# Keeping only the normalised rows in DRAM between router, expert blocks and combine, with four guessed experts

## The chip, the cores and the metric

The kernel runs on one core of one Trainium2 chip. The metric is the device time of one execution in microseconds; of the kernel before there are three timed runs and one profiled execution. Engine names: PE is the matrix engine (PEld its weight loads), DVE the vector engine, ACT the scalar engine, POOL the general-purpose engine, SP the engine that issues most DMAs. A name with q behind it (SPq, ACTq, POOLq) is that engine's instruction queue.

## The reference, cut to what matters

One decoder layer on 1024 tokens of width 1024: a mixer (gated DeltaNet heads and dilated attention heads), an output projection, a layer norm, a mixture of experts, a second layer norm. The change lies between the first norm and the end:

```python
x = layer_norm(ALPHA * x + (1 + gate1) * mix, ln1_g, ln1_b)
h = x * (1 + scale2) + shift2
lg = h @ w_rg + b_rg                     # 4 groups, the best one is taken
le = h @ w_re + b_re                     # 8 experts in it, the best two are taken
gates = softmax(lg)[grp] * softmax(top2(le))
hid = silu(h @ w_gate[e]) * (h @ w_up[e])   # 32 experts of width 512
y = sum over the two experts of gate * (hid @ w_down[e])
x = layer_norm(ALPHA * x + (1 + gate2) * y, ln2_g, ln2_b)
```

The first norm can be written as xh * ln1_g + ln1_b, where xh is the normalised row. So both h and ALPHA * x are a product and a sum of xh with rows that are the same for all tokens: h = xh * G2 + B2 and ALPHA * x = xh * L1G + L1B.

## The kernel before, in words

**Router stage.** After the mixer, eight tiles of 128 tokens go through two functions, `stage_a(n)` and `stage_b(n - 1)`, in the order `TORD` = 4, 5, 6, 7, 0, 1, 2, 3. `stage_a` finishes the output projection of its tile (`wo_gen`, PE: 48 products of 512 columns, whose moving operands are split in two parts by ACT, L861, and DVE, L863), adds the residual (DVE L1110, L1111), takes mean and variance (DVE L1116 to L1121, with the inverse root by POOL, L448) and writes xh by ACT (L1123). DVE then makes h2 (L1125, L1126), which SP stores to `h2d`; POOL makes ALPHA * x out of xh (L1128, L1129) and stores it to `x1d` (L1130). `stage_b` transposes h2 on PE (L1140), copies it by ACT (L1141), multiplies with the router weights (L128, pc), and `choose` and `places` on DVE (L1015 to L1044) find the two experts of each token and count.

**Guessed experts.** The 32 experts are dealt with in order of how many tokens they have. After four tiles `early` ranks them by what was counted so far; the experts at ranks 4 to 6 (`E0`, `NA` = 3) are loaded while the router still runs: one while the later tiles run, the two others into slots that come free as the stage ends.

**Slot tables.** Then ranks, block bases and slots are worked out (until about 800 us): `idxt` (row to gather per slot), `sct` (row to scatter to), `gat` (gate).

**MoE stage.** 81 static blocks of 32 slots run in the order `SEQ`, each for one expert. A block gathers its rows from `h2d` by POOL (`gather_x`, L1323; a tile of 128x256 holds 32 rows in quarters), PE transposes them (px, L1345), ACT copies (xT), PE multiplies with gate and up (ph, 64 products), ACT and DVE make th (L1359, L1360), PE transposes (pt, L1365), DVE copies (hT, L1367), PE multiplies with down (po, 32 products), DVE applies gate and gate2 (yo, L1378), POOL scatters to `y2d` (L1329). `y2d` has 2048 rows: one per token and choice. The weights stream through four gate/up slots (wgu, 4 MB each) and three down slots (wd, 2 MB each); SP issues a load when the slot's last user on PE is done.

**Surplus loop and end.** A loop (L1433) takes tokens beyond the static blocks; its count is read from memory, and it has no iterations on these inputs. The load of all `x1d` rows (L1486) stands ahead of it; the ln2 rows (L1490) and eight loads of `y2d` rows, 1 MB each (L1511), behind it. `combine` adds the two rows of a token to its x1 row, partly on PE (identity products, L128 ps), partly on DVE (L1517, L1530), ACT squares (L1533), `norm` finishes on DVE (L1540, L1541), and SP writes out (L1542).

A scheduler sets the order on each engine within the program's dependences; pools of buffers (`bufs`) set how far it can go ahead.

Of the kernel before, what the change touches and what calls it, by code (L numbers as in the profile page):

```python
# [20 lines left out]
P = 128  # L21
# [19 lines left out]
def const_tables():  # L41
# [36 lines left out]
    for k in range(2):  # L78
# [5 lines left out]
CAP_BLOCKS = [11, 9, 8, 6, 3, 3] + [2] * 11 + [1] * 12 + [3, 2, 2]  # L84
TE = 4
E0 = 4
NA = 3
# [7 lines left out]
ORDER = [29, 30, 31, 11, 3, 8, 7, 9, 25, 19, 22, 4, 2, 27, 14, 1, 5, 13, 18, 10, 21, 15, 0, 6, 16, 28, 17,  # L95
         12, 20, 26, 23, 24]
SEQ = [1, 1, 2, 2, 3, 3, 0, 0, 0, 5, 5, 4, 6, 6, 4, 7, 7, 4, 8, 4, 9, 4, 4, 10, 11, 11, 11, 12, 12, 12, 13,
       12, 12, 14, 14, 12, 12, 12, 15, 16, 16, 16, 17, 17, 15, 18, 15, 19, 19, 15, 20, 15, 15, 21, 21, 15,
       15, 15, 22, 23, 23, 22, 24, 24, 22, 25, 22, 26, 22, 22, 27, 27, 22, 28, 22, 29, 22, 22, 22, 30, 31]
# [24 lines left out]
def build(nc, tc, I, out):  # L124
# [7 lines left out]
    with es:  # L132
# [15 lines left out]
        h2d = dp.tile([S, D], F32, name="h2d")  # L148
        x1d = dp.tile([S, D], F32, name="x1d")
# [737 lines left out]

        def ln_step(i):
            if i == 1:
                for n_, src in (("G2", modd[2:3, :]), ("l1b", I["ln1_b"]), ("l1g", I["ln1_g"]), ("B2", modd[1:2, :])):  # L890
                    lc[n_] = row(lcp.tile([P, D], F32, name=n_), src)
            if i == LCI[0]:
                sb = lc["sb"] = bp.tile([P, NT, P], F32, name="PT", bufs=2).rearrange("p a b -> p (a b)")
                V.scalar_tensor_tensor(sb, lc["G2"], 1.0, lc["l1b"], op0=OP.add, op1=OP.mult)
                V.tensor_tensor(lc["B2"], lc["B2"], sb, op=OP.add)
            if i == LCI[1]:
                V.scalar_tensor_tensor(lc["G2"], lc["G2"], 1.0, lc["l1g"], op0=OP.add, op1=OP.mult)
            if i == 9:
# [40 lines left out]
        for h in range(H):  # L939
# [3 lines left out]
            if h == H - 1:  # L943
# [8 lines left out]
                lcp = wos.enter_context(tc.tile_pool(name="lcp", bufs=1, side="right", reuse_waits="tile"))  # L952
# [12 lines left out]
        sct = mp.tile([P, NB], I32, name="sct")  # L965
        eidi = mp.tile([1, NE], I32, name="eidi")
# [5 lines left out]
        V.tensor_scalar(g2t, g2t, 1.0, None, op0=OP.add)  # L972
        lt = mp.tile([P, NT, 36], F32, name="lt")
# [119 lines left out]

        def stage_a(n):
# [126 lines left out]
        for o_, c_, p0, p1_ in ((kr, cb, prede[:, 0], prede[:, 1]), (kc_, cc, predc[:, 0:1], predc[:, 1:2])):  # L1221
# [63 lines left out]
        gv = tl([P, 2, NT])  # L1285
# [84 lines left out]
        def block_d(pool, psp, hT, gcol, wd, b_, idx):  # L1370
# [7 lines left out]
            V.scalar_tensor_tensor(yo, po, gcol, g2t, op0=OP.mult, op1=OP.mult)  # L1378
            scatter_y(b_, idx, yo)
# [13 lines left out]
        ngu = nd = NA  # L1393
        fgu, fd = list(range(NA, 4)), list(range(NA, 3))
# [204 lines left out]
```

## Time and profile before

| | us |
|---|---|
| three timed runs | 1355.63, 1357.07, 1357.18 (median 1357.07) |
| the profiled execution | 1359.02 |
| its span | 1357.2 |
| busy in the span: PE, DVE, POOL, ACT | 1201.2, 616.0, 409.3, 335.1 |

The profile belongs to one execution, some 2 us slower than the median; its span is the time between its first and last recorded instruction. A row with a start is one instruction or a run of like ones. `[idle before <-releaser]` says how long the engine had been idle and what ended that. In a chain of work each piece is what the next one waited for, and "issue" is time for which no wait is on record.

### The profile page before, as it was taken

The page shows a single profiled execution, that of the slowest core. Times are in us where ns is not written, and L with a number is a line of the kernel's source. Part 1 is how long each engine was busy: PE and PEld are TensorE (multiplying, and loading weights), DVE is VectorE, ACT ScalarE, POOL GpSimd, SP SyncE. Part 2 cuts the span into 40 slices and gives each one's busy share as a digit, 9 for nine tenths or more (in the row PEclk, how much of TensorE's full clock was granted, in tenths as well). Part 3 has the DMA queues.
Part 4 walks back from the last instruction along what each step waited for, and adds up shares of the span by engine and source line. Part 5 has one row for each costly group of instructions (what it writes and reads, how often), then busy time and mean ns, then how long its engine had stood idle before and what let it go on. Part 6 is the DMA issues. An engine that isn't in the chain of part 4 may idle for free.

```text
span 1357.2 us, 32321 instructions
## 1 busy us (share of the span) xinstructions
PE 1201.2 (89%) x13901; PEld 813.3 (60%) x13901; DVE 616.0 (45%) x1404; ACT 335.1 (25%) x757; POOL 409.3 (30%) x396
## 2 busy tenths in 40 slices
PE   4898999999997989999988459999699999999956
PEld 0476777868785766867766335555355555555522
DVE  0859385674626747577987731111011111111126
ACT  1654343333322333344211101011011111111003
POOL 0223242332223404131532433333233333333113
PEclk8899999999998989999988659999899999999978
DMA  9210001110114335344436859999999999999965
GB/s 378 98 32 33 33 32 34 47 34 17 48 48 134 129 120 162 121 173 110 138 120 250 354 206 420 425 424 423 428 424 411 374 424 422 424 421 423 409 250 220
DMA packets 50629, 311.13 MB, mean 229 GB/s; under 512 B 10226, under 2 KB 18148, under 8 KB 40756
## 3 DMA queue, kind: packets, MB, share of 16 engines
q1 hardware_dynamic: 36064, 282.60, 52.1%
q0 software_dynamic: 8928, 21.00, 4.1%
q10 hardware_dynamic: 5492, 5.44, 1.2%
q8 instruction: 111, 1.82, 0.5%
q14 instruction: 34, 0.28, 0.1%
HBM read 286.56 MB, written 26.89 MB: 231 GB/s over the span
## 4 chain that ended last, share of the span: by engine, by line
PE 40%; DMA 11%; DVE 10%; issue 4%; POOL 3%; ACT 1%; POOLq 0%; SPq 0%; ACTq 0%; DVEq 0%
PE ph L128 17%; PE po L128 9%; DMA wd<-in_k_wd 8%; PE pj L128 5%; DMA araw<-in_w_ada 2%; PE pc L128 2%; PE pg L128 2%; PE pt L1365 1%; DVE acc L259 1%; PE px L1345 1%; POOL wlo L243 1%; DVE oh L1020 1%; DMA y2d<-yo,sct 1%; PE pg L787 1%; ACT sq L1533 1%
## 5 line engine op out<-in xcount | busy, mean ns | idle before, releaser
L128 PE MATMUL ph<-wgu,xT 128*32 128x256 f32 x5184 | 299.0, 383 | 0.0
L128 PEld LDWEIGHTS ph<-wgu,xT 128*32 128x32 f32 x5184 | 160.3, 110 | 113.7 <-issue 16.3
L128 PE MATMUL pj<-hhi,whi 128*128 128x512 f32 x448 | 193.5, 432 | 5.7 <-ACT akq L500 2.4
L128 PE MATMUL pj<-hlo,whi 128*128 128x512 f32 x448 | 181.5, 405 | 3.1 <-DVE hlo L234 2.9
L128 PE MATMUL pj<-hhi,wlo 128*128 128x512 f32 x448 | 180.9, 404 | 0.0
L128 PE MATMUL po<-wd,hT 128*32 128x256 f32 x2592 | 159.1, 387 | 18.0 <-DMA wd<-in_k_wd 17.5
L1323 POOL DMA_INDIRECT xg<-h2d,idxt x81 | 82.6, 1020 | 273.2 <-PE px L1345 265.9
L1360 DVE TENSOR_TENSOR th<-th,ph 128x128 f32<-128x128 f32 x81 | 23.3, 288 | 303.2 <-ACT th L1359 303.2
L243 POOL TENSOR_TENSOR wlo<-wraw,whi 128x256 fp32r<-128x256 f32 x112 | 96.4, 891 | 205.0 <-ACT whi L240 158.5
L128 PEld LDWEIGHTS po<-wd,hT 128*32 128x32 f32 x2592 | 85.5, 112 | 76.6 <-issue 21.2
L1329 POOL DMA_INDIRECT y2d<-yo,sct x81 | 82.0, 1012 | 67.8 <-DVE hT L1367 42.0
L128 PEld LDWEIGHTS pj<-hhi,whi 128*128 128x128 f32 x448 | 85.5, 191 | 23.1 <-ACT akq L500 2.8
L128 PEld LDWEIGHTS pj<-hlo,whi 128*128 128x128 f32 x448 | 85.7, 191 | 20.0 <-DVE hlo L234 7.6
L128 PEld LDWEIGHTS pj<-hhi,wlo 128*128 128x128 f32 x448 | 85.4, 191 | 17.2 <-issue 0.9
L1378 DVE SCALAR_TENSOR_TENSOR yo<-po,gat,g2t 128x256 f32<-128x256 f32 x81 | 39.2, 484 | 115.2 <-PE po L128 115.2
L1359 ACT ACTIVATE th<-ph 128x128 f32<-128x128 f32 x81 | 22.5, 278 | 262.2 <-PE ph L128 262.2
L1347 ACT COPY xT<-px 128x256 f32<-128x256 f32 x81 | 30.2, 373 | 205.0 <-PE px L1345 205.0
L128 PE MATMUL pg<-akq 128*128 128x512 f32 (+3 forms) x96 | 40.7, 539 | 10.2 <-DVE sm L772 6.1
L128 PE MATMUL pj<-wohi,mhi 128*128 128x512 f32 x112 | 46.8, 418 | 0.0
L128 PE MATMUL pj<-wo,mhi 128*128 128x512 f32 x112 | 45.7, 408 | 0.0
L128 PE MATMUL pc<-vtk,PT 128*128 128x128 f32 x288 | 39.2, 281 | 6.6 <-ACT PT L789 6.4
L128 PE MATMUL pj<-wohi,mlo 128*128 128x512 f32 x112 | 45.0, 402 | 0.0
(698 smaller groups left out, 1784.0 us busy)
## 6 DMA issues: line engine op xcount, KB each, us to landing
wgu<-in_k_wgu SPq DMA_DIRECT2D x32, 4096.0 KB, 16.7
wd<-in_k_wd SPq DMA_DIRECT2D x32, 2048.0 KB, 23.7
araw<-in_w_ada SPq DMA_DIRECT2D x32, 512.0 KB, 4.0
wraw<-in_k_win SPq DMA_DIRECT2D x28, 512.0 KB, 3.5
wad<-in_w_ada SPq DMA_DIRECT2D x8, 1024.0 KB, 10.3
wgu<-y2d SPq DMA_DIRECT2D x8, 1024.0 KB, 11.1
xT<-in_k_xt SPq DMA_DIRECT2D x4, 1024.0 KB, 18.4
xr<-in_x SPq DMA_DIRECT2D x8, 512.0 KB, 4.8
```

What stands on the lines that cost most here:

```text
L128: return T.matmul(o, l, r, start=start, stop=stop)
L243: G.tensor_tensor(lo[:, k:k + 2], raw[:, k:k + 2], hi[:, k:k + 2].bitcast(F32), op=OP.subtract)
L259: V.scalar_tensor_tensor(state["acc"], raw, sc[:, k:k + 1], state["acc"], op0=OP.mult, op1=OP.add)
L787: T.transpose(p[:, b_ - b0, :], sc_[:, b_ * P:(b_ + 1) * P], ident)
L1020: V.tensor_scalar(o_, e_, f_, None, op0=OP.is_equal)
L1323: G.indirect_dma_start(out=xg, out_offset=None, in_=h2v, in_offset=bass.IndirectOffsetOnAxis(ap=idx, axis=0), bounds_check=4 * S - 1, oob_ ...
L1329: G.indirect_dma_start(out=y2v[b_], out_offset=bass.IndirectOffsetOnAxis(ap=idx, axis=0), in_=yo, in_offset=None, bounds_check=8 * S - 1, ...
L1345: pe(T.transpose(px[:, hh, :], xg[:, hh * P:(hh + 1) * P], ident))
L1347: A.copy(xT, px)
L1359: A.activation(th, ph[:, 0], AF.Silu)
L1360: V.tensor_tensor(th, th, ph[:, 1], op=OP.mult)
L1378: V.scalar_tensor_tensor(yo, po, gcol, g2t, op0=OP.mult, op1=OP.mult)
```

## The change

1. `h2d` and `x1d` go; SP stores xh alone (`xhd`). DVE's L1125 and L1126 and POOL's L1128, L1129, L1130 go with them, as do the four row loads and their five operations in the attention stage.
2. The router multiplies xh with weights that have G2 folded in, and B2's product is added to the bias (`router_weights`, once).
3. The four rows G2, B2, L1G, L1B are loaded in the blocks' layout (`lns`, sixteen small DMAs by ACT).
4. Each expert block makes h2 out of its gathered xh (`block_h2`) and ALPHA * x (x1 in `block_d`); a block's row that holds a token's first choice (`fst` is 1) gets x1 added to yo. The combine then has two rows to add, not three. xg has 7 buffers in place of 6, yo 4 in place of 7, xT 2 in place of 3; the program gathers 4 blocks ahead in place of 5.
5. Four experts are guessed (`NA` = 4); the fourth one's gate and up weights are loaded into the fourth slot ahead of the MoE stage. `ORDER`, `SEQ` and `CAP_BLOCKS` are new tables of the same kind.
6. The eight `y2d` row loads stand ahead of the surplus loop, and are repeated at the end of each of its iterations. Sums of three of the tiles are made on PE and ACT, of five on DVE.

```diff
-CAP_BLOCKS = [11, 9, 8, 6, 3, 3] + [2] * 11 + [1] * 12 + [3, 2, 2]
+CAP_BLOCKS = [11, 9, 8, 6, 3, 3] + [2] * 10 + [1] * 12 + [3, 2, 2, 2]
-NA = 3
+NA = 4
-SEQ = [1, 1, 2, 2, 3, 3, 0, 0, 0, 5, 5, 4, 6, 6, 4, 7, 7, 4, 8, 4, 9, 4, 4, 10, 11, 11, 11, 12, 12, 12, 13,
+SEQ = [2, 2, 1, 1, 0, 0, 0, 3, 4, 5, 4, 3, 4, 4, 4, 4, 7, 6, 8, 6, 9, 8, 9, 8, 10, 8, 11, 10, 8, 12, 8, 12, 8,
...
+        def ln_consts(k, w):
+            V.scalar_tensor_tensor(w, k[:, G2], 1.0, k[:, L1B], op0=OP.add, op1=OP.mult)
+            V.tensor_tensor(k[:, B2], k[:, B2], w, op=OP.add)
+            V.scalar_tensor_tensor(k[:, G2], k[:, G2], 1.0, k[:, L1G], op0=OP.add, op1=OP.mult)
...
+        def lns_load(j, src):
+            for q in range(4):
+                A.dma_start(lns[32 * q:32 * q + 32, j], src[:, 256 * q:256 * q + 256].to_broadcast([32, 256]))
+        def lns_step(n):
+            if n < 4:
+                lns_load(n, (modd[2:3, :], modd[1:2, :], I["ln1_g"], I["ln1_b"])[n])
...
+        def router_weights():
...
+            V.tensor_tensor(brt, brt, pb[:, 0:36], op=OP.add)
+            V.tensor_tensor(wr[:, :, 0:36], wr[:, :, 0:36], lkc[:, 0, :, None].to_broadcast([P, KD, 36]), op=OP.mult)
...
             A.activation(xh, r_, AF.Identity, bias=mv[:, 4:5], scale=mv[:, 3:4])
-            h2 = lp.tile([P, D], F32, name="h2", bufs=2)
-            V.tensor_tensor(r_, xh, lc["G2"], op=OP.mult)
-            V.tensor_tensor(h2, r_, lc["B2"], op=OP.add)
-            (SY if n < NT - 1 else A).dma_start(h2d[ts, :], h2)
-            G.tensor_tensor(xh, xh, lc["l1g"], op=OP.mult)
-            G.tensor_tensor(xh, xh, lc["l1b"], op=OP.add)
-            G.dma_start(x1d[ts, :], xh)
-            return h2
+            (SY if n < NT - 1 else A).dma_start(xhd[ts, :], xh)
+            return xh
...
+        def block_h2(pool, xg):
+            h2 = pool.tile([P, 256], F32, name="h2", bufs=2)
+            V.tensor_tensor(h2, xg, lns[:, G2], op=OP.mult)
+            V.tensor_tensor(h2, h2, lns[:, B2], op=OP.add)
+            return h2
...
+        def block_d(pool, psp, hT, gcol, wd, b_, idx, xg, fcol):
+            x1 = pool.tile([P, 256], F32, name="x1", bufs=1)
+            V.tensor_tensor(x1, xg, lns[:, L1G], op=OP.mult)
+            V.tensor_tensor(x1, x1, lns[:, L1B], op=OP.add)
...
             V.scalar_tensor_tensor(yo, po, gcol, g2t, op0=OP.mult, op1=OP.mult)
+            V.scalar_tensor_tensor(yo, x1, fcol, yo, op0=OP.mult, op1=OP.add)
...
         down(nb - 1)
+        yall = [ring(fgu[j]).rearrange("p (t k d) -> p t k d", t=4, k=2) for j in range(2)]
+        y2r = y2d.rearrange("(k t p) d -> t p k d", k=2, p=P)
+        def load_rows():
+            for t in range(NT):
+                SY.dma_start(yall[t // 4][:, t % 4], y2r[t])
+        load_rows()
         overflow()
```

What the diff alone doesn't show is where the scheduler puts these instructions. The first place is ACT's queue at the start of the router stage (lns: the new constants; brt: the router's bias; mhi: the split operand of the output projection; hT: the transposed rows). Before:

```order
L970 DMA g2t<-modd 32x256 x4
L1091 DMA brt<-in_b_router_group 128x4
L1092 DMA brt<-in_b_router_expert 128x32
L861 CAST mhi<-mraw 128x896
L1123 ACTIVATE xh<-r__6198,mv 128x1024
L861 CAST mhi<-mraw 128x896
L1141 COPY hT<-pg 128x512 x2
L1123 ACTIVATE xh<-r__6255,mv 128x1024
```

and now:

```order
L1079 DMA brt<-in_b_router_expert 128x32
L1095 DMA lns<-modd 32x256 x4
L860 CAST mhi<-mraw 128x896
L1147 ACTIVATE xh<-r__6191,mv 128x1024
L1095 DMA lns<-modd 32x256 x4
L1095 DMA lns<-in_ln_g 32x256 x4
L1095 DMA lns<-in_ln_b 32x256
L860 CAST mhi<-mraw 128x896
L1095 DMA lns<-in_ln_b 32x256
L1159 COPY hT<-pg 128x512 x2
L1095 DMA lns<-in_ln_b 32x256 x2
L1147 ACTIVATE xh<-r__6262,mv 128x1024
```

Four of the sixteen loads now stand ahead of the first tile's cast and xh, ten ahead of its hT copies, and the others ahead of the second tile's xh. Each waits on one of eight semaphores that SP's and ACT's DMAs share in turn.

The second place is DVE in the middle of the MoE stage, one block and a half. Before:

```order
L1378 SCALAR_TENSOR_TENSOR yo<-po,gat,g2t 128x256
L1367 COPY hT<-pt 128x128
L1360 TENSOR_TENSOR th<-th,ph 128x128
L1378 SCALAR_TENSOR_TENSOR yo<-po,gat,g2t 128x256
L1367 COPY hT<-pt 128x128
```

and now (h_ is h2 of the block two ahead, x_ the x1 of the block whose yo comes next):

```order
L1424 SCALAR_TENSOR_TENSOR yo<-po,gat,g2t 128x256
L1409 COPY hT<-pt 128x128
L1425 SCALAR_TENSOR_TENSOR yo<-x_10105,fst,yo 128x256
L1380 TENSOR_TENSOR h_10235<-xg,lns 128x256
L1415 TENSOR_TENSOR x_10194<-xg,lns 128x256
L1381 TENSOR_TENSOR h_10235<-h_10235,lns 128x256
L1416 TENSOR_TENSOR x_10194<-x_10194,lns 128x256
L1402 TENSOR_TENSOR th<-th,ph 128x128
L1424 SCALAR_TENSOR_TENSOR yo<-po,gat,g2t 128x256
L1409 COPY hT<-pt 128x128
```

Five operations have come between hT and the next th.

The third place is SP at the end, from the last weight load on (wgu names the slot that is reused for the rows). Before:

```order
L1486 DMA wgu_13347<-x1d 128x8x1024 [waits DMAHW2_49]
L1433 COMPARE_AND_BRANCH
L1433 UNCONDITIONAL_BRANCH
...
L1490 DMA wd_13545<-in_ln_g 128x1024
L1490 DMA wd_13545<-in_ln_b 128x1024
L1511 DMA wgu_13869<-y2d 128x2x1024 [waits DMASW5_49]
```

and now:

```order
L1544 DMA wd_14087<-in_ln_g 128x1024 [waits DMAHW3_49,PE_49]
L1544 DMA wd_14087<-in_ln_b 128x1024 [waits DMAHW2_49]
L1560 DMA wgu_14182<-y2d 128x2x1024 [waits DMASW4_49,DMASW5_49,DMASW3_49,DMASW6_49,DMASW2_49,DMASW7_49,DMASW1_49,DMASW0_49]
L1560 DMA wgu_14182<-y2d 128x2x1024 [waits DMAHW4_49]
...
L1483 COMPARE_AND_BRANCH
L1483 UNCONDITIONAL_BRANCH [waits DMAHW0_49,DMAHW1_49,DMAHW2_49,DMAHW3_49,DMAHW4_49,DMAHW5_49,DMAHW6_49,DMAHW7_49]
```

The row loads stand ahead of the loop's branches; the branch that goes round the loop (the second row of L1483) now waits on all eight semaphores of SP's DMAs, where it had no wait before. On POOL the last eight scatters now stand ahead of its loop branches, where the last one stood behind.

## Rows read from the trace of the kernel before

**Rows 1.** Windows: stretch, length, busy per engine (instructions), clock, DMA share, GB/s

```profile
675.25:692.50 17.25, 15.02 (x77) 12.01 (x76) 14.64 (x33) 3.36 (x4) 7.01 (x5) 0.90 0.34 119
785.00:800.00 15.00, 5.23 (x34) 4.81 (x34) 6.38 (x17) 0.00 (x0) 3.48 (x8) 0.50 0.20 87
815.00:1265.00 450.00, 435.71 (x7361) 248.19 (x7357) 72.57 (x225) 48.35 (x149) 148.60 (x146) 0.98 1.00 418
```

**Rows 2.** Chain of work in the router stage: start, length, piece

```profile
698.48 1.40 PE pg L1140 x8
750.33 3.41 POOL xh L1128
757.94 0.58 POOL mv L448
768.84 1.93 PE pc L128 x16
```

**Rows 3.** Timelines of DVE and POOL in one router tile: start, length, instruction

```profile
691.94 2.38 DVE L1017 SCALAR_TENSOR_TENSOR e<-lem,m,kc 128x32 f32<-128x32 f32 x1
695.05 1.72 DVE L1020 TENSOR_SCALAR oh<-e,f__6646 128x32 f32<-128x32 f32 x1
697.25 0.25 DVE L1017 SCALAR_TENSOR_TENSOR e<-lem,m,kc 128x32 f32<-128x32 f32 x1
690.84 3.43 POOL L1128 TENSOR_TENSOR xh<-xh,l1g 128x1024 f32<-128x1024 f32 x1 [4.42 <-DVE r__6522 L1125]
```

**Rows 4.** ACT's g2t loads by line (ns min/median/max), then its timeline

```profile
L970 ACTq DMA_DIRECT2D g2t<-modd x4: 432/444/1971, 635.0 to 638.0; - x4
635.01 3.39 ACTq L970 DMA_DIRECT2D g2t<-modd  x4
639.40 0.94 ACT L861 CAST mhi<-mraw 128x896 fp32r<-128x896 f32 x1 [5.22 <-DMA g2t<-modd]
```

**Rows 5.** Timelines in the MoE stage: PE (start, then one block), DVE, POOL

```profile
802.41 0.66 PE L1345 MATMUL px<-kc,xg 128*128 128x128 f32 x2 [5.23 <-DMA xg<-h2d,idxt]
1003.30 0.33 PE L1365 MATMUL pt<-kc,th 128*128 128x128 f32 x1
1009.10 0.33 PE L1365 MATMUL pt<-kc,th 128*128 128x128 f32 x1
1002.02 0.29 DVE L1360 TENSOR_TENSOR th<-th,ph 128x128 f32<-128x128 f32 x1 [3.70 <-ACT th L1359]
1004.12 1.02 POOL L1323 DMA_INDIRECT xg<-h2d,idxt  x1 [3.45 <-PE px L1345]
1005.45 1.01 POOL L1329 DMA_INDIRECT y2d<-yo,sct  x1 [0.31 <-issue]
```

**Rows 6.** PE's waits in the stage, SP's first loads, gathers from issue to landing

```profile
PE po L128 <- DMA wd<-in_k_wd: 17.5, 5, 9.9
804.98 9.88 SPq L988 DMA_DIRECT2D wgu<-in_k_wgu  x2
DMA to landing us min/median/max: 2.7/9.4/11.9
```

**Rows 7.** The end: DVE's and SP's timelines, the chain, groups of operations

```profile
1300.76 0.48 DVE L1378 SCALAR_TENSOR_TENSOR yo<-po,gat,g2t 128x256 f32<-128x256 f32 x1 [2.06 <-PE po L128]
1314.20 1.23 DVE L1517 TENSOR_TENSOR wgu<-wgu 128x1024 f32<-128x1024 f32 x1 [12.96 <-DMA wgu<-y2d]
1309.34 6.67 SPq L1511 DMA_DIRECT2D wgu<-y2d  x8
1303.54 5.78 DMA y2d<-yo,sct
1351.14 1.28 DVE wgu L1541
L1540 DVE SCALAR_TENSOR_TENSOR wgu<-wgu,mv,wd 128x1024 f32<-128x1024 f32 x8 | 10.2, 1281 | 0.0
L1530 DVE CUSTOM_DVE_ANT_0 wgu<-wgu,wgu 128x1024 f32<-128x1024 f32 x2 | 2.4, 1223 | 0.0
```

More of the change, by code (lines that the diff above doesn't have):

```diff
@@ L147, in build @@
         modd = dp.tile([4, D], F32, name="modd")
-        h2d = dp.tile([S, D], F32, name="h2d")
-        x1d = dp.tile([S, D], F32, name="x1d")
+        xhd = dp.tile([S, D], F32, name="xhd")
         y2d = nc.dram_tensor("y2d", [2 * S, D], F32)[:, :]
@@ L965, in build @@
         sct = mp.tile([P, NB], I32, name="sct")
+        fst = mp.tile([P, NB], F32, name="fst")
         eidi = mp.tile([1, NE], I32, name="eidi")
@@ L972, in build @@
         V.tensor_scalar(g2t, g2t, 1.0, None, op0=OP.add)
+        lns = mp.tile([P, 4, 256], F32, name="lns")
+        G2, B2, L1G, L1B = range(4)
         lt = mp.tile([P, NT, 36], F32, name="lt")
@@ L1092, in build @@
         A.dma_start(brt[:, 4:36], I["b_router_expert"].to_broadcast([P, 32]))
+        lnk = lp.tile([KD, 4, P], F32, name="lnk")
+        for j, src in enumerate((modd[2:3, :], modd[1:2, :], I["ln1_g"], I["ln1_b"])):
+            SY.dma_start(lnk[:, j], src.rearrange("o (k p) -> (o k) p", p=P))
+        lnw = lp.tile([P, 256], F32, name="lnw")
+        def ln_consts(k, w):
+            V.scalar_tensor_tensor(w, k[:, G2], 1.0, k[:, L1B], op0=OP.add, op1=OP.mult)
+            V.tensor_tensor(k[:, B2], k[:, B2], w, op=OP.add)
+            V.scalar_tensor_tensor(k[:, G2], k[:, G2], 1.0, k[:, L1G], op0=OP.add, op1=OP.mult)
+        ln_consts(lnk, lnw[0:KD, 0:P])
+        def lns_load(j, src):
[4 more added lines that the diff above has]
+                lns_load(n, (modd[2:3, :], modd[1:2, :], I["ln1_g"], I["ln1_b"])[n])
+            if n == 6:
+                ln_consts(lns, lnw)
+                V.tensor_scalar(lns[:, L1G:L1B + 1], lns[:, L1G:L1B + 1], ALPHA, None, op0=OP.mult)
+        def router_weights():
+            pk = pch()
+            for j, c_ in ((G2, 0), (B2, KD)):
+                T.transpose(pk[:, c_:c_ + KD], lnk[:, j], ident[0:KD, 0:KD])
+            lkc = lp.tile([P, 2, KD], F32, name="lkc")
+            V.tensor_copy(lkc, pk[:, 0:2 * KD].rearrange("p (j k) -> p j k", j=2))
+            pb = pch()
+            for k in range(KD):
+                mm(pb[:, 0:36], lkc[:, 1, k:k + 1].to_broadcast([P, P]), wr[:, k, 0:36], start=(k == 0), stop=(k == KD - 1))
+            V.tensor_tensor(brt, brt, pb[:, 0:36], op=OP.add)
+            V.tensor_tensor(wr[:, :, 0:36], wr[:, :, 0:36], lkc[:, 0, :, None].to_broadcast([P, KD, 36]), op=OP.mult)
         def stage_a(n):
@@ L1177, in build @@
             h2n = stage_a(n)
+            if n == 0:
+                router_weights()
+            lns_step(n)
             if n > 1:
@@ L1195, in build @@
         wpools["wgu2"] = wpools["wd2"] = wqb
-        for i in range(1, NA):
+        for i in range(1, 3):
             load_gu(i, i, eid_reg(eide, E0 + i))
             load_d(i, i)
+            if i == 2:
+                wqc = mes.enter_context(tc.tile_pool(name="wqc", bufs=1, side="right", reuse_waits="tile"))
+                wpools["wgu3"] = wqc
+                load_gu(3, 3, eid_reg(eide, E0 + 3))
         rts = ExitStack()
@@ L1284, in build @@
         V.scalar_tensor_tensor(gs[:, 2], gs[:, 1], 1.0, gs[:, 0], op0=OP.add, op1=OP.mult)
-        gv = tl([P, 2, NT])
+        gv = rtk.tile([P, 2, NT], F32, name="gv")
         V.reciprocal(gv[:, 0], gs[:, 2])
@@ L1392, in build @@
         b0s = [b_ // BT_ for b_ in BASES]
-        ngu = nd = NA
-        fgu, fd = list(range(NA, 4)), list(range(NA, 3))
+        ngu, nd = NA, NA - 1
+        fgu, fd = [], []
         left = [CAP_BLOCKS[r] for r in ORDER]
@@ L1446, in overflow @@
                 V.tensor_copy(gcl[:, 0:1], pc_[:, 1:2])
+                first(gcl[:, 3:4], ic[:, 3:4], ic[:, 0:1])
                 V.tensor_scalar(gcl[:, 1:2], ctr, float(-NB), None, op0=OP.add)
@@ L1464, in build @@
             G.memset(xp_.tile([P, 256], F32, name="xg", bufs=XB), 0.0)
-        for n in range(XB - 1):
+        for n in range(LG):
             gx(n)
@@ L1483, in build @@
                     break
-            if nd == NE and fgu and xall is None:
-                xall = ring(fgu.pop(0)).rearrange("p (t d) -> p t d", d=D)
-                SY.dma_start(xall, x1d.rearrange("(t p) d -> p t d", p=P))
             if nd == NE and fd and lnb is None:
```

113 lines of the change are left out of this document (51 added, 62 removed).

## The prediction

> **What bounds the kernel now.** I read the windows by stage first, then the chain of work through the router stage, then single engines' timelines where a term needs one. The windows [rows 1] show four regimes. In the router stage (633 to 769 us) a steady token tile takes 17.25 us, in which PE is busy 15.02 at clock 0.90 and DVE 14.64: neither is full, so the two wait for each other. In the MoE stage (802 to 1301) PE is busy 435.71 of 450 us while the DMA share is 1.00 at 418 GB/s: two limits at nearly the same height. In the last 56 us (1301 to 1357) the row loads and then DVE's operations of 1.28 us set the pace [rows 7]. The slot tables between (769 to 802) are a chain of small operations that the change leaves as it is.
>
> The chain through the router [rows 2] shows what the tile waits for: the transposes of h2 (PE pg L1140) stand behind DVE and POOL, and in the later tiles POOL's L1128 (3.41 us at 750.33) lies in the chain itself, with POOL's small mv (757.94) waiting its turn behind it. DVE's rows [rows 3] show why DVE is so full: L1017 takes 2.38 us while POOL's L1128 runs, and 0.25 us with POOL free; L1020, of the same kind, takes 1.72 beside L1129.
>
> **The change part by part.** The profiled execution took 1359.02 us with a span of 1357.2, so 1.8 lie around the span; it stands 1.95 above the median of 1357.07. I sum against the span, and take the difference from the median at the end.
>
> *Router stage, removed.* Each tile loses DVE L1125 and L1126 (2 x 1.2 us), POOL L1128 (3.43 us), L1129 and the x1d issue, and the stretch of L1017 and L1020, (2.38 - 0.25) + (1.72 - 0.25) = 3.6 us [rows 3]. L1125 and L1126 are costed by the combine's sum of the same size, 1.23 us [rows 7]. DVE falls from 14.6 to 14.6 - 2.4 - 3.6 = 8.6 us a tile, so PE is late next. PE's 15.02 us at clock 0.90 would be 13.5 at the full 2.4 GHz [rows 1]; I take 14.3 a tile, midway. That is 2.95 less than 17.25. From the transposes of the fourth tile at 698.48 to the last router product at 768.84 [rows 2] are 70.4 us for four tiles, so 4 x 2.95 = 11.8; in the last tile mv no longer stands behind the previous tile's POOL pair, 750.33 to 757.94 or 7.6 us instead of one tile's 2.95, so 4.7 more. The three tiles before give 3 x 2.95 = 8.9.
>
> *Router stage, added.* The eight loads of G2 and B2 rows become small: four by SP and sixteen of 32x256 (lns) on ACT's queue. The nearest row: g2t's four issues have a median of 0.444 us and a longest of 1.97, and ACT's next cast waited 5.22 us [rows 4]. Behind the sixteen stand, on ACT, the casts of mhi for the output projection, xh and the hT copies; PE waits for these. Four lie before the first cast and xh(0), ten before hT(0). Bounds: 16 x 0.444 = 7 us and 16 x 1.97 = 32; I take 0.85 each (g2t's four from 635.01 took 3.39), which makes hT(0) some 7 us late (twelve to fourteen issues, less the wait of ACT that they fill), less 2.4 as h2 is gone: about 5 us once. The router weights (two transposes, eight products, two DVE operations) cost about 1 us, under the same stall. So the stage ends 11.8 + 4.7 + 8.9 - 5 - 1 = 19.4 us sooner; I take 18, since some waits on DVE stay, and bounds of 8 (the pace shrinks by one operation only) and 24 (no stall). The constants' work taken out of the last attention stretch, on DVE, ACT and SP, is hidden beside PE: 0 to 3, I take 1.
>
> *Fourth guessed expert.* Its 4.19 MB are read in the gap before the MoE stage, where DMA moves 87 GB/s [rows 1]: 10.0 us at the 418 GB/s of the stage behind it, free if it ends before the first gathers, up to 3 us if not; I take 1.5. The start of the stage also gets h2's two products, x1's first and a seventh memset: four operations of 0.3 to 0.5, 1.5 us. Together +3.
>
> *MoE stage.* PE's pace is 5.80 us a block (1003.30 to 1009.10, [rows 5]), 81 blocks or 469.8 us; the stage took 498.3, from the first px at 802.4 [rows 5] to the last po at 1300.7, just ahead of the last yo [rows 7]. Of the other 28.5 us po waited 17.5 for wd [rows 6]; about 11 are a first block at half clock, slower clock behind the stalls, and the end. The transfers, 182.5 MB of weights (29 experts of 6.29 MB) and 21.2 MB of gathered and scattered rows (162 of 0.131), need 487 us at 418 GB/s: the stalls are those of a stream with little slack. After, 4.19 MB less are to come, but the stream starts later: before, a slot was free and it began at 804.98 [rows 6]; after, all four slots are full, and the first comes free when the first expert's two blocks have left gate and up, about 8.3 us into the stage. 8.3 + 199.5/0.418 = 486: the saving and the late start nearly cancel at the floor, but the work in hand at the start is one expert more, which covers early stalls. I expect 11 to 12 us of stalls in place of 17.5: -6, bounds -10 and +3.
>
> Five DVE operations of 128x256 come into each block (h2, x1, and the sum into yo), at about 0.33 each, between th's 0.29 [rows 5] and yo's 0.48 [rows 7]: 1.65 us. In each block DVE is idle 3.70 us before th [rows 5], so they fit. The scatter leaves 0.33 us later and the gather stands behind x1; with gathers landing in at most 11.9 us [rows 6] and seven buffers, four blocks or 23 us lie between issue and use. Cost 0.
>
> What the DVE rows do beside POOL [rows 3] speaks against this cover: POOL issues a gather and a scatter, 1.02 and 1.01 us, in just that idle stretch [rows 5]. Two holds of that length make 1.65 + 2.03 = 3.68 of 3.70 us, so still free, and th, done at 1002.31, has another 1.0 us until its transpose at 1003.30. The Trainium skill, "SBUF — State Buffer", section "SBUF: two separate sides", says that an operation with two SBUF inputs and one on GpSimd exclude each other for the whole instruction; that agrees with L1017, and no row here shows it for a DMA issue. It would take effect only with longer holds; that is rival 4.
>
> *The end.* Before, the last scatter stood behind the surplus loop: yo was done at 1301.24, the scatter issued at 1303.54, landed 5.78 us later, and the row loads began at 1309.34 [rows 7]. After, the scatter stands before the loop: yo's end, r (0.33), issue and landing give 1307.4. But all eight loads now stand before the loop too, and on the way round it SP waits for all eight and the exit holds every engine for SP. So the combine that began at 1314.20 with the first rows [rows 7] can't begin until 8.39 MB have landed: 20.1 us at 418 GB/s and 1 to start, 1328.5; through the loop another 2.3 (as 1301.24 to 1303.54 before), 1330.8. By the Trainium skill, "DMA: Bandwidth & Descriptors", section "Where 436 GB/s comes from", reads from HBM are held to about 358 GB/s, which would make these loads 23.4 us and the end 3.3 later; the 418 GB/s held over 450 us [rows 1] speak against it, and the sum keeps 418. Then DVE's own work is left bare: 16 operations of 1.28, five sums of 1.22 [rows 7], and sixteen tiny ones of about 0.15, 29 us, with first and last steps on ACT and POOL 32: 1362.8. From the last DVE operation (1351.14 + 1.28) to the end are 4.8 us: 1367.6 against 1357.2, +10. Bounds +5 (the combine's DVE packs without gaps, a quick loop) and +14.
>
> *Sum:* -1 - 18 + 3 - 6 + 10 = -12: span 1345, own time 1347, and 12 below the median: **1345 us**.
>
> **The rivals.**
> 1. *The loop doesn't hold the combine*: the wait at SP's branch may concern earlier transfers only. Then the end is 2 us sooner than before in place of 10 later: 1333. For it: nothing runs between loads and combine that needs the loop. Against: the order of SP shows the wait on all eight lanes of its queue, which before hadn't one.
> 2. *ACT's sixteen issues cost more than the router gains.* Place: ACT ahead of xh(0) and hT(0). At 1.97 us each [rows 4], fourteen take 28 instead of 12 us, 15 net more: 1360, slower than before. It decides from about 1.7 us an issue. For it: each waits for an earlier transfer of its lane. Against: g2t's median.
> 3. *The MoE stage gains nothing*: the late start of the stream eats the saved bytes, +0 to +3 in place of -6: 1351 to 1354.
> 4. *Holds between DVE and POOL in the MoE stage.* If an issue holds DVE as long as L1017 was held, 2.13 us, a block has 1.65 + 4.26 = 5.9 for 4.7 of room: 1.2 x 81 = 97 us, less 15 of stalls it hides: about 1427. Against it: the issues themselves last 1.0 us [rows 5], half of that. What the Trainium skill says in the section cited above is its mechanism.
> 5. *The router tiles keep their pace*: DVE's chain of small operations sets it, not the big ones, and only 8 are won: 1355, no change to speak of.
>
> **How the numbers follow.** Forecast 0.57, rivals 0.10, 0.10, 0.13, 0.03 and 0.07 in that order. The range reaches from rival 1 to just short of rival 2: 1333 to 1358, since the bounds of router (-24 to -8), MoE (-10 to +3) and end (+5 to +14) seldom all fall on one side. A measurement of this kernel tells 0.2% (2.7 us) from no change. Faster: the forecast, rival 1, nearly all of 3, a little of 5, 0.80. Same: most of 5 and a bit of 2 and 3, 0.07. Slower: 2, 4, and the forecast's worst corner, 0.13.
>
> **What would show it.** Router: tiles at 14 to 14.5 us with L1017 at 0.25 throughout, and the last router product near 750. A first tile with ACT held over 15 us on lns would be rival 2. MoE: th still waited for by ACT alone, stalls on wd under 15 us, block pace 5.80. End: a stretch of some 20 us with no engine busy while rows land, and DVE then at over 90%. I am wrong if DVE starts the combine within 15 us of the last po, if the router's tiles stay over 16 us, or if po waits for wd over 25 us.

## The result: 25 us faster, twice the forecast

| | us |
|---|---|
| kernel before, median | 1357.09 |
| changed kernel, four runs | 1331.42, 1331.80, 1332.42, 1334.79 (median 1332.11) |
| ratio, 95% interval | 0.9828 [0.981, 0.9846] |
| profiled execution of the changed kernel, its span | 1331.80, 1329.6 |

The direction was right. The size was not: 25 us against the 12 forecast, and the median lies 0.9 us under the low end of the stated range. The spans differ by 27.6 us, the medians by 25.0 (the profiled execution of the kernel before is 2 us above its median). Four marks divide the spans (the last router product on PE, the first px, the first operation on the last yo, the end):

| piece | before | after | difference | forecast |
|---|---|---|---|---|
| to the last router product | 768.8 | 738.8 | -30.0 | -19 |
| from there to the first px | 33.6 | 37.6 | +4.0 | +3 |
| MoE stage, to the last yo | 498.4 | 491.1 | -7.2 | -6 |
| from there to the end | 56.4 | 62.1 | +5.7 | +10 |

So the two middle pieces came out near the forecast in size. The router gave 11 us more, and the end took 4 us less.

### The profile page after: what moved, and what is told of

Same layout as the page of the kernel before. It is cut to its first block, busy times and chain, and to the rows that moved or that the text cites. A ratio compares the mean times of both kernels' runs of the same rounds, so it can differ in the third digit from the quotient of the medians.

```text
span 1329.6 us, 32637 instructions
## 1 busy us (share of the span) xinstructions
PE 1175.5 (88%) x13879; PEld 802.4 (60%) x13879; DVE 712.3 (54%) x1802; ACT 331.6 (25%) x753; POOL 377.3 (28%) x373
## 5 line engine op out<-in xcount | busy, mean ns | idle before, releaser
L1365 POOL DMA_INDIRECT y2d<-yo,sct x81 | 102.6, 1267 | 287.3 <-DVE yo L1425 287.3
L128 PEld LDWEIGHTS po<-wd,hT 128*32 128x32 f32 x2592 | 85.8, 111 | 70.4 <-issue 11.3
L1402 DVE TENSOR_TENSOR th<-th,ph 128x128 f32<-128x128 f32 x81 | 23.3, 288 | 164.6 <-ACT th L1401 164.6
L1359 POOL DMA_INDIRECT xg<-xhd,idxt x81 | 83.8, 1035 | 26.1 <-issue 25.9
L447 POOL TENSOR_TENSOR mv<-mv,pio 128x1 f32<-128x1 f32 x16 | 14.4, 900 | 142.4 <-DVE mv L1143 86.3
L258 DVE SCALAR_TENSOR_TENSOR acc<-araw,sc,acc 128x1024 f32<-128x1024 f32 x28 | 37.5, 1339 | 14.0 <-DMA araw<-in_w_ada 13.9
```

Source lines behind the costliest of these rows:

```text
L128: return T.matmul(o, l, r, start=start, stop=stop)
L258: V.scalar_tensor_tensor(state["acc"], raw, sc[:, k:k + 1], state["acc"], op0=OP.mult, op1=OP.add)
L447: G.tensor_tensor(o, x, e.to_broadcast(list(x.shape)), op=OP.pow)
L1359: G.indirect_dma_start(out=xg, out_offset=None, in_=xhv, in_offset=bass.IndirectOffsetOnAxis(ap=idx, axis=0), bounds_check=4 * S - 1, oob_ ...
L1365: G.indirect_dma_start(out=y2v[b_], out_offset=bass.IndirectOffsetOnAxis(ap=idx, axis=0), in_=yo, in_offset=None, bounds_check=8 * S - 1, ...
L1402: V.tensor_tensor(th, th, ph[:, 1], op=OP.mult)
```

## The profile after

First the marks, on PE's timeline of the changed kernel (start, length, instruction): the transposes of two tiles that follow each other, the last router product, the first px.

```profile
674.23 1.07 PE L1158 MATMUL pg<-kc,xh 128*128 128x128 f32 x8
687.69 1.07 PE L1158 MATMUL pg<-kc,xh 128*128 128x128 f32 x8
738.75 1.98 PE L128 MATMUL pc<-hT,wr 128*64 128x128 f32 x16
776.35 0.66 PE L1387 MATMUL px<-kc,h 128*128 128x128 f32 x2 [9.50 <-DVE eidi L1526]
```

The tiles follow each other at 13.46 us, where the steady tile of before took 17.25 [rows 1].

Then the start of the router, on PE's timelines: the last transposes of the attention stage and the router's first, before, and the same two now, with the products of the router weights between.

```profile
632.82 0.63 PE L811 MATMUL pg<-kc,ob 128*128 128x128 f32 x4 [1.10 <-DVE ob L807]
646.94 1.03 PE L1140 MATMUL pg<-kc,h 128*128 128x128 f32 x8
```

```profile
630.81 0.63 PE L810 MATMUL pg<-kc,ob 128*128 128x128 f32 x4 [1.10 <-DVE ob L806]
639.59 1.95 PE L128 MATMUL pc<-wr,lkc 128*128 128x36 f32 x16 [0.18 <-issue]
647.60 1.04 PE L1158 MATMUL pg<-kc,xh 128*128 128x128 f32 x8
```

So the 30.0 us of the first piece have three parts. The stage begins 2.0 us sooner, but nothing can be read from that: in the nine profiled kernels that have the changed kernel's code up to there it begins anywhere from 628.5 to 636.6. Its first transposes come 16.8 us after that start in place of 14.1, or 2.7 later, with PE busy all the way (14.00 of the 14 us from 633 in the kernel before, 16.82 of the 17 from 631 now). From the first transposes to the last product are 91.2 us in place of 121.8, a gain of 30.7 in the tiles.

The windows of the changed kernel (columns as in [rows 1]) show the steady tile, the MoE stage and the stretch after the last scatter.

```profile
675.25:692.50 17.25, 17.13 (x103) 13.52 (x102) 12.67 (x37) 4.04 (x6) 0.54 (x1) 1.00 0.35 114
805.00:1230.00 425.00, 413.29 (x6993) 236.47 (x6985) 190.18 (x563) 45.88 (x142) 162.69 (x141) 0.99 1.00 416
1268.00:1295.00 27.00, 0.00 (x0) 0.00 (x0) 0.48 (x1) 0.00 (x0) 0.98 (x1) 0.55 0.79 313
```

In the same 17.25 us PE is busy 17.13 where it had 15.02, and the clock is 1.00 where it was 0.90 [rows 1]; POOL's 7.01 us of work are down to 0.54. In the last window no engine computes more than next to nothing for 27 us (DVE 0.48, POOL's 0.98 is the last scatter's issue). DVE's short operation that took 2.38 us beside POOL [rows 3] (now L1004, ns min/median/max) is never held:

```profile
L1004 DVE SCALAR_TENSOR_TENSOR e<-lem,m,kc x16: 250/252/255, 655.7 to 744.9; 128x32 f32<-128x32 f32 x16
```

The end, on DVE's, POOL's and SP's timelines, and two windows of it:

```profile
1267.48 0.48 DVE L1424 SCALAR_TENSOR_TENSOR yo<-po,gat,g2t 128x256 f32<-128x256 f32 x1 [1.51 <-PE po L128]
1295.04 1.23 DVE L1583 CUSTOM_DVE_ANT_0 wgu<-wgu 128x1024 f32<-128x1024 f32 x1 [26.56 <-SPq L1483]
1324.58 1.28 DVE L1593 SCALAR_TENSOR_TENSOR wgu<-wgu,mv,wd 128x1024 f32<-128x1024 f32 x1
1268.76 0.98 POOL L1365 DMA_INDIRECT y2d<-yo,sct  x1 [2.38 <-DVE yo L1425]
1271.76 4.91 SPq L1560 DMA_DIRECT2D wgu<-y2d  x8
1276.00:1292.00 16.00, 0.00 (x0) 0.00 (x0) 0.00 (x0) 0.00 (x0) 0.00 (x0) 0.50 1.02 417
1294.00:1295.00 1.00, 0.00 (x0) 0.00 (x0) 0.00 (x0) 0.00 (x0) 0.00 (x0) 0.50 0.00 0
```

The row loads are issued 4.3 us after the last yo begins, but DVE waits 26.56 us, and what it waits for is SP at the loop's line. That is the wait that the order of SP showed. The rows move at 417 GB/s, and by 1294 no transfer is left; only then, at 1295.04, DVE begins. Before, DVE began as the first rows landed [rows 7].

In the MoE stage, PE's wait for down weights and one stretch of DVE and POOL:

```profile
PE po L128 <- DMA wd<-in_k_wd: 13.0, 6, 4.8
1034.41 0.29 DVE L1402 TENSOR_TENSOR th<-th,ph 128x128 f32<-128x128 f32 x1 [1.96 <-ACT th L1401]
1031.38 1.28 POOL L1365 DMA_INDIRECT y2d<-yo,sct  x1 [3.18 <-DVE yo L1425]
```

Po's 17.5 us of waits [rows 6] are 13.0 now. DVE is idle 1.96 us before th, where it was 3.70 [rows 5], so the five operations take 1.74. The scatter's issue takes 1.28 us where it took 1.01 [rows 5].

## Experiments

### Which of the removed operations freed the router

Theory: POOL's two long operations held DVE and the small mv. Rival: DVE's own two operations were the load. Three kernels: the first takes only POOL's pair out of the kernel before, the second only DVE's, the third puts a POOL pair back into the changed kernel (a shorter one: 1.9 and 2.4 us, where the removed pair took 3.4 and 2.4).

e2_before_no_pool, on the kernel before:

```diff
-            G.tensor_tensor(xh, xh, lc["l1g"], op=OP.mult)
-            G.tensor_tensor(xh, xh, lc["l1b"], op=OP.add)
```

e3_before_no_h2, on the kernel before:

```diff
-            V.tensor_tensor(r_, xh, lc["G2"], op=OP.mult)
-            V.tensor_tensor(h2, r_, lc["B2"], op=OP.add)
-            (SY if n < NT - 1 else A).dma_start(h2d[ts, :], h2)
-            G.tensor_tensor(xh, xh, lc["l1g"], op=OP.mult)
-            G.tensor_tensor(xh, xh, lc["l1b"], op=OP.add)
-            G.dma_start(x1d[ts, :], xh)
-            return h2
+            (SY if n < NT - 1 else A).dma_start(h2d[ts, :], xh)
+            G.tensor_tensor(h2, xh, lc["l1g"], op=OP.mult)
+            G.tensor_tensor(h2, h2, lc["l1b"], op=OP.add)
+            G.dma_start(x1d[ts, :], h2)
+            return xh
```

e7_pool_back, on the changed kernel:

```diff
+            px_ = lp.tile([P, D], F32, name="px_", bufs=1)
+            G.tensor_tensor(px_, xh, xh, op=OP.mult)
+            G.tensor_tensor(px_, px_, xh, op=OP.add)
```

e2_before_no_pool, expected:

> The kernel before without POOL's two operations on xh (L1128, L1129) in the router stage: the residual's constants are left out, and x1d gets xh itself. Theory (POOL's long operations stretch DVE's and hold back mv, and the clock is low because PE waits): tile period from 17.25 to 14.6 us or less, clock above 0.95, the last router product 12 to 25 us earlier, total 1332 to 1345. Rival (DVE's own two operations of 128x1024 are the bound): 0 to 5 us faster, 1352 to 1357.

e3_before_no_h2, expected:

> The kernel before without DVE's two operations on xh (L1125, L1126): h2 is xh, so the second scale and shift are left out; POOL's two operations stay (they write a tile of their own). Theory (POOL is the larger part): DVE still stretched, tile period 15 to 16.5 us, 3 to 10 us faster in all, 1347 to 1354. Rival (DVE's own work is the bound): 12 us or more faster, under 1345.

e7_pool_back, expected:

> The changed kernel with two POOL operations of 128x1024 put back into each router tile, reading xh and writing a tile that nobody reads. Theory (POOL's operations were what slowed the router): 8 to 20 us slower than the changed kernel, 1340 to 1352, with L1004 at over 2 us in each tile and a clock under 1.0 in the stage. Rival (with DVE's two operations gone there is room enough): under 3 us slower, below 1335.

Measured: 1330.37 us (ratio to before 0.9774 [0.9753, 0.9795]), 1376.51 (1.0118 [1.0098, 1.0139]) and 1344.98 (0.9885 [0.9858, 0.9911]). First e2, PE's timeline (first transposes, last product) and a window in the steady tiles:

```profile
645.84 1.03 PE L1138 MATMUL pg<-kc,h 128*128 128x128 f32 x8
740.39 1.77 PE L128 MATMUL pc<-hT,wr 128*64 128x128 f32 x16
660.00:690.00 30.00, 29.86 (x176) 23.65 (x175) 25.40 (x70) 7.45 (x10) 2.26 (x4) 1.00 0.41 139
```

Without POOL's pair alone the last product is at 740.4: 28.4 of the router's 30 us (27.3 of the 30.7 in the tiles), more than the 12 to 25 expected. The clock is 1.00, and the total is no longer than that of the changed kernel (0.9774 of the kernel before, against 0.9828). DVE's two operations still run there, so taking them away adds little once POOL is out. No short operation on DVE is held in e2; how much of the gain is theirs and how much is that of the small mv behind POOL's pair was not separated.

Then e3 and e7, each with the first transposes and the last product on PE; of e3 the instruction that tells why its total can't be read (a group by line: count, busy, mean ns), and of e7 the transposes of the fourth and the fifth tile, two waits of PE, DVE's L1007 in one tile and the window around the fifth tile.

```profile
646.50 1.03 PE L1138 MATMUL pg<-kc,xh 128*128 128x128 f32 x8
751.20 1.98 PE L128 MATMUL pc<-hT,wr 128*64 128x128 f32 x16
L1452 POOL DMA_INDIRECT wgu<-in_k_wgu,ic x1 | 1.0, 982 | 4.5 <-DMA wgu<-x1d 4.5
```

```profile
649.72 1.03 PE L1161 MATMUL pg<-kc,xh 128*128 128x128 f32 x8
691.49 1.07 PE L1161 MATMUL pg<-kc,xh 128*128 128x128 f32 x8
705.13 0.18 PE L128 MATMUL pc<-Mc,onesb 128*128 128x32 bf16 x1 [3.46 <-DVE Mc L1024]
712.97 1.07 PE L1161 MATMUL pg<-kc,xh 128*128 128x128 f32 x8
751.87 0.19 PE L128 MATMUL pc<-Mb,striub 128*128 128x32 bf16 x1 [4.60 <-DVE Mb L1020]
752.01 1.98 PE L128 MATMUL pc<-hT,wr 128*64 128x128 f32 x16
687.25 2.20 DVE L1007 TENSOR_SCALAR oh<-e,f__6659 128x32 f32<-128x32 f32 x1
690.00:720.00 30.00, 26.41 (x138) 19.72 (x137) 21.70 (x68) 6.52 (x8) 5.36 (x5) 0.89 0.41 156
```

In e3 the last product is 17.6 us earlier than before, at 751.2 (17.1 in the tiles). Its total is longer because h2 without scale and shift sends tokens to other experts: the surplus loop ran once (L1452 is in its body). Only its router stage is evidence. The steady tiles follow each other at 14.0 us (674.47 to 688.47), where 15 to 16.5 were expected, and 17 us is more than the theory's 3 to 10 and lies where the rival had it: DVE's own two operations were a load nearly as large as POOL's pair. The larger part is POOL's, as stated, but only by 27 to 17.

In e7 the last product is at 752.0, 13.3 later than in the changed kernel, of which 2.1 lie ahead of the first transposes and 11.1 in the tiles; the total is longer by 8 us (by the ratios) to 13 (by the medians), as the theory had it. L1007, of the same kind as the L1020 of before, is held 2.20 us again, and L1004 in seven of its sixteen instances, but the steady tiles still follow each other in 13.5 us: with DVE's pair gone there is room for the hold. What is lost is lost mainly at two places. The fifth tile, ahead of which four tiles' counts are ranked, comes 21.5 us after the fourth (712.97 after 691.49; 15.2 in the changed kernel), and PE waits there 3.46 us for the held chain on DVE. At the last tile PE waits 4.60 us for the chain of small operations. So the savings overlap: in the tiles POOL's pair 27, DVE's pair 17, both 31.

### ACT's sixteen issues

```diff
-                A.dma_start(lns[32 * q:32 * q + 32, j], src[:, 256 * q:256 * q + 256].to_broadcast([32, 256]))
+                SY.dma_start(lns[32 * q:32 * q + 32, j], src[:, 256 * q:256 * q + 256].to_broadcast([32, 256]))
```

> The changed kernel with the sixteen small lns loads issued by SP instead of ACT. Theory (ACT's queue delays the first tile's hT by little, PE has other products to run): 0 to 2 us faster, 1330 to 1333. Rival (ACT's queue holds the router's start, as the prediction had it with 5 us): 3 to 6 us faster, 1326 to 1329.

Measured: 1335.05 us, 0.982 [0.9794, 0.9847]; the changed kernel's 0.9828 lies inside. The last transposes of the attention stage and the router's first (630.81 and 647.60 in the changed kernel):

```profile
630.98 0.63 PE L810 MATMUL pg<-kc,ob 128*128 128x128 f32 x4 [1.10 <-DVE ob L806]
647.61 1.04 PE L1158 MATMUL pg<-kc,xh 128*128 128x128 f32 x8
```

The way between the two is 16.6 us in place of 16.8, and the last product (738.75 and 738.89) did not move either. In the changed kernel ACT's sixteen issues had taken 0.31 to 0.78 us each, a median near 0.43, and PE was busy 29.01 of the 30 us from 630 to 660: it had other products to run. The 5 us of the prediction for this queue were 0.

### The MoE stage

Four kernels. One loads the fourth guessed expert late; one goes back to three guessed experts with the orders of before; one leaves out the five DVE operations; one does four of them twice.

e4_gu3_late:

```diff
-                load_gu(3, 3, eid_reg(eide, E0 + 3))
...
+        load_gu(3, 3, eid_reg(eidi, ORDER[3]))
         for n, (i, b_) in enumerate(blocks):
```

e8_three_guessed, which also has CAP_BLOCKS, ORDER and SEQ of before:

```diff
-NA = 4
+NA = 3
...
-                load_gu(3, 3, eid_reg(eide, E0 + 3))
...
-        ngu, nd = NA, NA - 1
-        fgu, fd = [], []
+        ngu = nd = NA
+        fgu, fd = list(range(NA, 4)), list(range(NA, 3))
```

e5_lean_blocks:

```diff
-            V.tensor_tensor(h2, xg, lns[:, G2], op=OP.mult)
-            V.tensor_tensor(h2, h2, lns[:, B2], op=OP.add)
-            V.tensor_tensor(x1, xg, lns[:, L1G], op=OP.mult)
-            V.tensor_tensor(x1, x1, lns[:, L1B], op=OP.add)
-            V.scalar_tensor_tensor(yo, x1, fcol, yo, op0=OP.mult, op1=OP.add)
```

e9_double_ops, and the same for the two operations on x1:

```diff
             V.tensor_tensor(h2, xg, lns[:, G2], op=OP.mult)
             V.tensor_tensor(h2, h2, lns[:, B2], op=OP.add)
+            V.tensor_tensor(h2, xg, lns[:, G2], op=OP.mult)
+            V.tensor_tensor(h2, h2, lns[:, B2], op=OP.add)
```

e4_gu3_late, expected:

> The changed kernel, but the fourth guessed expert's gate and up weights are loaded at the start of the MoE stage (with the numbers the gathers wait for), not in the gap ahead of it. Theory of the prediction (one expert more in hand is worth 6 us to the stage and costs 3 to 4 at its start): the way to the first px gets 3.5 us shorter, the stage 6 longer, total about 1335. Rival (saved bytes and late start of the stream cancel): the stage stays within 1 us, total about 1329.

e8_three_guessed, expected:

> The changed kernel with three guessed experts, and with the orders, caps and first loads of the kernel before; the rest of the change stays. The late load of the fourth expert's weights cost the MoE stage only 0.5 us, so the 7 us that the stage won lie elsewhere. Theory (the new block order and the fourth guess together): the stage, first px to last yo, goes back to 496 to 499 us from 491, the waits of po for wd to 17 us, total 1336 to 1340. Rival (the x1d reads and the shorter scatter traffic that are gone): the stage stays at 490 to 492, total 1330 to 1333.

e5_lean_blocks, expected:

> The changed kernel without the five added DVE operations of each expert block: blocks use the gathered normalised rows as they are and the residual is not added to yo, so that part of the computation is left out. Theory (they lie in DVE's idle time): total 1330 to 1333, the MoE stage within 2 us of 491. Rival (holds between DVE and POOL, or the later scatters, cost the stage): 3 us or more faster.

e9_double_ops, expected:

> The changed kernel with h2 and x1 of each block computed twice, so four more DVE operations of 128x256 a block, some 1.35 us where 1.96 us of DVE's idle time are left ahead of th. Theory (the added operations lie in idle time): the stage within 2 us of 491, total 1330 to 1334. Rival (DVE's operations or holds with POOL cost the stage part of their length): 10 us or more slower.

Measured: 1333.76, 1336.78, 1331.56 and 1335.05 us; ratios 0.9822, 0.9816, 0.98 and 0.9814, with intervals that all hold the changed kernel's 0.9828. So the totals do not decide, and the stage's own marks must (first px and the operation on the last yo; stage in the changed kernel 776.35 to 1267.48, 491.1 us). How far such marks move by themselves is seen in e1, e6, e7 and e10, which have the changed kernel's tables, gap and blocks: with the changed kernel, their stages are 489.7 to 491.2 us, and from the last router product to the first px are 36.7 to 37.8.

e4, timelines of PE and DVE and the wait of po:

```profile
775.86 0.66 PE L1386 MATMUL px<-kc,h 128*128 128x128 f32 x2 [8.36 <-DVE eidi L1525]
1267.46 0.48 DVE L1423 SCALAR_TENSOR_TENSOR yo<-po,gat,g2t 128x256 f32<-128x256 f32 x1 [1.79 <-PE po L128]
PE po L128 <- DMA wd<-in_k_wd: 11.5, 5, 4.0
```

491.6 us: the early load of the fourth expert is worth 0.5 us to the stage. The way to the first px got 0.75 us shorter (36.8), not 3.5. Both are no more than the spread of kernels that have the early load, so no price of it is seen: the saved bytes and the late start of the stream cancel, as the rival had it. The rival's total of 1329 did not come, as it had counted on the 3.5.

e8, the same rows:

```profile
781.13 0.66 PE L1386 MATMUL px<-kc,h 128*128 128x128 f32 x2 [8.22 <-DVE eidi L1525]
1278.54 0.48 DVE L1423 SCALAR_TENSOR_TENSOR yo<-po,gat,g2t 128x256 f32<-128x256 f32 x1 [0.80 <-PE po L128]
PE po L128 <- DMA wd<-in_k_wd: 17.8, 7, 9.7
```

497.4 us, and the wait is back at 17.8. So of the 7 us that the stage won, 6 come with the new tables and the fourth guess together, and by e4 not through the time at which the fourth expert is loaded. That leaves the tables of caps and order; but they were not put back alone, so this is a conclusion by subtraction, and which entry does it was not tried. (The router stage of this run began 5.7 us later than that of the changed kernel, so only its MoE stage is compared.)

e5 and e9, the last yo of each, of e5 PE's wait, a block on PE, and its scatters by line (ns min/median/max), and of e9 the first px and a gather's issue:

```profile
1266.85 0.48 DVE L1418 SCALAR_TENSOR_TENSOR yo<-po,gat,g2t 128x256 f32<-128x256 f32 x1 [2.25 <-PE po L128]
PE po L128 <- DMA wd<-in_k_wd: 1.1, 2, 0.8
1002.06 0.33 PE L1404 MATMUL pt<-kc,th 128*128 128x128 f32 x1
1007.95 0.33 PE L1404 MATMUL pt<-kc,th 128*128 128x128 f32 x1
L1365 POOL DMA_INDIRECT y2d<-yo,sct x81: 980/1017/1028, 794.0 to 1267.6; - x81
```

```profile
1030.57 1.30 POOL L1359 DMA_INDIRECT xg<-xhd,idxt  x1 [0.72 <-DVE x L1419]
775.49 0.66 PE L1389 MATMUL px<-kc,h 128*128 128x128 f32 x2 [10.59 <-DVE h L1383]
1268.18 0.48 DVE L1428 SCALAR_TENSOR_TENSOR yo<-po,gat,g2t 128x256 f32<-128x256 f32 x1
```

e5's stage is 489.8 us from its first px at 777.01, e9's 492.7 from 775.49. Four more operations in each of 81 blocks, some 110 us of DVE's time, cost 1.6 us, hardly more than the spread: the theory holds, the added operations lie in idle time. In e5 po hardly waits, but its blocks take 5.89 us on PE in place of 5.80, so no more is won than 1.3 us, within the spread. Why they take longer, with the clock at 1.00, stays open.

### The end

e1_rows_behind; the first line taken out is the call at the end of an iteration of the surplus loop:

```diff
-                load_rows()
...
-        load_rows()
         overflow()
         xes.close()
+        load_rows()
```

e10_rows_behind_sums has the same and this, by which PE and ACT, not DVE, make the sums of two more tiles:

```diff
-        ASUM = (1, 3, 5)
+        ASUM = (1, 2, 3, 5, 6)
```

e1_rows_behind, expected:

> The changed kernel with one thing undone: the eight row loads stand behind the surplus loop again, as they did before. Theory (the loop holds the combine until all rows have landed): DVE starts the combine within 15 us of the last yo instead of 27.6, the end shrinks from 62 us to about 53, total about 1323 us. Rival (loads ahead of the loop are a gain, and the end is long because of the combine's own work): the loads start 4 to 5 us later, total 1334 to 1337.

e10_rows_behind_sums, expected:

> The changed kernel with the row loads behind the loop, as in e1_rows_behind, and five of the eight sums of the combine on PE and ACT in place of three. Theory (with rows streaming in, DVE's own 30 us set the end): DVE loses two sums of 1.3 us, 1 to 3 us faster than e1_rows_behind. Rival (the landing of the rows sets it, or ACT becomes late): within 1 us of it, or slower.

Measured: 1316.68 us, 0.9697 [0.9665, 0.9729], and 1320.79, 0.9695 [0.9655, 0.9735]. e1's timelines of SP and DVE:

```profile
1266.27 0.48 DVE L1424 SCALAR_TENSOR_TENSOR yo<-po,gat,g2t 128x256 f32<-128x256 f32 x1 [1.77 <-PE po L128]
1276.67 1.23 DVE L1582 CUSTOM_DVE_ANT_0 wgu<-wgu 128x1024 f32<-128x1024 f32 x1 [9.40 <-DMA wgu<-y2d]
1271.31 4.74 SPq L1559 DMA_DIRECT2D wgu<-y2d  x8
```

The loads are issued 5.0 us after the last yo begins, 0.8 later than in the changed kernel. DVE begins 5.4 us after that, with the first rows, and waits for DMA, not for SP at the loop. The end takes 47.8 us in place of 62.1, and the kernel is 15 us faster than the changed one: with the same rows, bytes and sums, only the place of eight issues differs. The theory holds, and e1 beats both kernels; the end is 5 us shorter than the 53 expected, with a combine of 37.4 us where it took 43.0 before (one row a token fewer to add). e10 gained nothing over e1, so its theory fails: from its first DVE operation of the combine (1283.84) to the end it took 38.2 us, e1 37.4, so DVE's own work alone does not set this piece.

## Why the prediction was right, and where it was not

**Router, removed work: right mechanism, a term too small.** Rows 2 and 3 pointed at POOL's pair, and e2 shows it: 27 of the 31 us in the tiles. The mis-sized term is the pace of 14.3 us a tile, "midway" between 13.5 and 15.0. It was 13.46. With PE hardly waiting the clock stayed at 1.00 (2.4 GHz), so the lower bound was the value to take: seven tiles by 0.8 are 6 us. Against that stands that no pace is the same for all tiles, as the sum assumed: before, they followed each other at 14.2 to 21.3 us, and the fifth still takes 15.2. In the sum's own pieces, the three tiles to the fourth one's transposes gave 11.3 us for the forecast 8.9, and the rest to the last product 19.4 for 16.5.

**Router, added work: the term failed.** It had 5 us for ACT's issues and 1 for the router weights, 6 in all; it was 2.7. e6 shows 0 for the issues, as PE had other products queued. For the same reason the router weights cost more than 1: their products stand on a PE that was full already, and the first transposes come 2.7 us later. The 3.3 us that were charged too much here, the 2.4 and 2.9 of the tiles, the 1.4 by which 19.4 was taken down to 18, and the 1.0 by which the stage began earlier still than forecast make the 11 us by which the router was under-forecast. That last one is chance. The stated bound of 24 was passed for these reasons.

**Gap and fourth expert: the total right, the parts wrong.** +4.0 against +3. The load of the fourth expert, forecast at 1.5, has no price that the runs show: without it (e4) the gap is 36.8 us, and with it 36.7 to 37.8. By the timelines, POOL's seven memsets now wait for fst, and the first gather is issued 0.9 us later after the last router product (31.3 in place of 30.4). Its rows are used 4.9 us after the issue (770.09 to 774.97) in place of 3.2, which no run explains; and px then stands 1.4 us behind h2, the first operation on x1, and eidi.

**MoE stage: right size, wrong reason.** -7.2 against -6. The fourth expert in hand, on which the term rested, is worth 0.5 us, which is not told from nothing; some 6 us go with the tables and the fourth guess together (e8), by subtraction the tables. That the size came out is luck. That DVE's five operations cost nothing was right, at 1.74 us a block against the 1.65 assumed.

**Holds between DVE and POOL (rival 4).** It had its place in the trace, and no price: the scatter's issue went from 1.01 to 1.28 us and back to 1.02 in e5 without the added operations, and in e9, where operations on h2 and x1 run beside it, the gather's issue takes 1.30 us. It was POOL that was held, not DVE as the rival had it: the first of the added operations is as long in all its 81 instances (changed kernel, ns min/median/max).

```profile
L1380 DVE TENSOR_TENSOR h<-xg,lns x81: 406/418/426, 775.0 to 1242.0; 128x256 f32<-128x256 f32 x81
```

The Trainium skill, "SBUF — State Buffer", section "SBUF: two separate sides", has a DVE operation with two SBUF inputs and a GpSimd operation that reads SBUF exclude each other. The scatters are in line with it, with 0.27 us a block, which POOL's idle time takes.

**The end: right mechanism, over 4 us too dear.** DVE waited for SP at the loop as stated, and from the issue of the loads to the start of the combine were 23.3 us where the prediction's terms make 23.4; the 418 GB/s that the sum kept held, at 417. Too dear were the scatter's landing (the loads began 4.3 us after the last yo began, not 6.6), the combine (30.8 us, not 32) and what follows the last operation (3.7 us, not 4.8).

**Rival 1 named the measured time and is false.** It gave 1333 us by an end 2 us shorter than before. The end is 5.7 us longer. A reader of the total alone would have taken it for confirmed; the 26.56 us on DVE's row, and e1, say otherwise.

## What to carry to other kernels

An engine that looks half idle (POOL here) can hold another through its long operations and through a small operation queued behind them: look at the longest instance of a short operation, not at its mean. A wait that is cheap when nothing is in flight becomes dear when transfers are issued ahead of it: before moving loads ahead of a loop, even one of no iterations, see what its branches wait for. When two removals each free the same limit, their savings do not add: here taking out two POOL operations a tile (e2) brought as much as the whole change, and the change with its loads behind the loop (e1) some 15 us more.

## What was not expected of the hardware

The granted clock: 0.90 in steady tiles with PE busy 15.02 of 17.25 us [rows 1], a mean between stretches at 2.4 GHz and at 1.2; 1.00, all at 2.4 GHz, with 17.13 of the same 17.25 now, and in e2 with 29.86 of 30. In e7's window around the fifth tile, with PE busy 26.41 of 30, it was 0.89. In these rows the stretches with waits lose their length and show a lower clock too.
